# A meta-key split of its own, a row addition ahead of weight conversions, and a last accumulation ahead of another tile's output

## The chip, the cores and the metric

The kernel runs on one core of one Trainium2 chip. The metric is the device time of one execution in microseconds (us). The kernel before takes 1303.13 us, the median of 3 runs (1301.97 to 1304.59). One more execution was recorded with the hardware profiler; it took 1304.39 us, and its records span 1302.6 us.

## The reference

The reference is one encoder block over 16 learned meta tokens, a prompt of 512 rows and a sample of 256 rows, all of width 1024; both row groups use the same weights, and the meta rows are dropped from the output:

```
n1   = rmsnorm(h)
proj = n1 @ w_in                      # S5 input | q | k | v | retention gate | merge gates A, B
a    = GLU(gelu(S5(u)))               # bidirectional complex diagonal state
o    = retention(rope(q), rope(k), v) # 4 heads, chunkwise recurrent, both directions
state0[h] = sum_s km[s] vm[s] gf^(15-s)                # the 16 meta positions start the state
b    = (rmsnorm(o) * silu(gate)) @ w_ret_out
h    = h + (sigmoid(gate_a) * a + sigmoid(gate_b) * b) @ w_out
n2   = rmsnorm(h)
h    = h + (silu(n2 @ w_gate) * (n2 @ w_up)) @ w_ffn_out     # width 2816
out  = rmsnorm(h)[16:]
```

Three places of this matter here: the term `state0`, which needs the 16 meta keys of each head; the residual sum after `w_out` with the norm `n2` behind it; and the final norm.

## The kernel before

All matrix products run in a split form. An fp32 operand x is turned into a high part (`hi`, written by ScalarE, line 101, in the matmul type fp32r) and a low part (`lo` = x - hi, by VectorE or GpSimd, line 89), and a product is three matmuls: hi by hi, the cross term lo by hi, and hi by lo (lines 81, 82, 83 are one such triple; line 1114 is another place that issues them). Weights are converted 128 x 512 at a time by `convert` (line 162): `whi` on ScalarE, then `wlo` on VectorE. Converted weights lie in a ring of six pairs (`WH = 6`), raw weights in a ring of three tiles `wraw` (`WR = 3`). The class `Ops` (lines 178 to 196) is a queue over the conversions in a fixed sequence: `fill(n)` converts until n pairs wait in the queue, `next()` hands one out and fills up to `ahead` again. Some steps of the sequence carry a sum of weight quarters as well (`wraw<-wraw` on GpSimd), because the projections in pairs are done by a Strassen-Winograd scheme with seven products for eight; the operands `n20` to `n26` of the trace are the seven operands of that scheme on the activations.

Through nearly all of the program each engine works in the order in which the code is written (`manual_schedule`). An instruction that waits holds up all that stands behind it on its engine.

**Retention.** The four heads run from about 300 to 490 us. What one head does is a list of calls named by the string `SEQ` (line 48): `KS` splits the rotated keys, `VM` the meta values, `KT` turns the weighted keys and splits them, and also turns, weights and splits the 16 meta keys (`kmw`, `kmhi`, `kmlo`), `V0` to `V2` split the values (their low parts `vlo` on GpSimd), `ST` multiplies keys by values into the states, `S0` to `S2` form the scores (`sr`, then `sThi` and `sTlo`), and each `F` is one product of the gate projection, with the weight conversions that it causes and the copies and sums that take its result out of PSUM (`q`, `u`, `c`). The products `F` are not part of the retention; they fill TensorE while the head's own work goes through the other engines. `ws.ahead` is 4 here.

**Between w_out and the FFN.** The six row tiles of 128 rows take the second half of `w_out` one after the other (`col_half`, eight weight pairs `wos`, of which the first four lie in the ring and the last four in a pool of their own). After each tile its sum is added to the residual (`add_half`: `hres<-bank,hres`), ScalarE squares it (`row_stats`), GpSimd makes the reciprocal root, VectorE scales it (`scale_rows`: `nx<-hres,rstd,gffn`), TensorE transposes it (line 1877), and `rows_first` or `rows_second` form the FFN's operands from the transposed tile. Tile i is scaled inside the work on tile i - 1, at the place `mid`. In between the first FFN weights are converted by `ws.fill`. Then four products of FFN units 1 and 2 (`pre`), the last tile's transposes, and two products of unit 0 follow; from about 820 us the FFN proper runs.

**The end.** The last group of the FFN's second projection leaves three sums that arrive one after the other (i = 0, 1, 2). `accumulate(P4, i)` adds one to the residual, `second_half` takes the norm of row tile 3 + i, and `finish` scales a finished tile and issues its output DMAs. The last two outputs (`rows_out(5, ...)`) end the program.

Of the kernel before, what the change touches and what calls it, by code (L numbers as in the profile page):

```python
# [16 lines left out]
D = 1024  # L17
# [3 lines left out]
NT = SP + SS  # L21
NA = NT + NM
KT = D // 128
# [21 lines left out]
RS = ((1, 1, 1, 0), (1, 1, 1, 1), (1, 1, 0, 1), (1, 1, 1, 1))  # L45
DE = ((1, 1, 1, 1), (1, 1, 0, 1), (1, 1, 1, 1), (1, 1, 0, 1))
VLP = (0, 1, 2)
SEQ = 'B Z0 A D KS VM F V0 KL QD F C F F V1 F V2 KT S2 F F KU ST QL KR F F O2 S1 VL F Z2 F QU S0 O1 QR F DL Z1 QS F O0 F ZL'
HALF = 3.84
E_T = (0, 0.794)  # L50
R_T = (13, 0.997)
# [9 lines left out]
def build(nc, tc, I, O):  # L61
    V = nc.vector
    A = nc.scalar
    P = nc.gpsimd
    T = nc.tensor
# [11 lines left out]
    def raw(t):  # L77
        return t.bitcast(F32)
# [9 lines left out]
    def tt(e, out, a, b, op):  # L88
        e.tensor_tensor(out=out, in0=a, in1=b, op=op)  # L89

    def ts(e, out, a, s1, op0, s2=None, op1=None):
        if op1 is None:
            e.tensor_scalar(out=out, in0=a, scalar1=s1, scalar2=None, op0=op0)  # L93
        else:
            e.tensor_scalar(out=out, in0=a, scalar1=s1, scalar2=s2, op0=op0, op1=op1)  # L95
# [4 lines left out]
    def act(out, a, f, **kw):  # L100
        A.activation(out=out, in_=a, func=f, **kw)  # L101
# [40 lines left out]
    ident = cp.tile([128, 128], F32, name="ident")  # L142
# [71 lines left out]
    def weights():  # L214
        for i in range(NPLAIN):
            yield from plain(i, P if i == 3 else V)
        for i in range(12):
            yield from units.pop(i) if i in units else pair_unit(i)
        rq = [ret_unit(44 + 2 * i) for i in range(4)]
        for op in ("p1", "p5", "p2", "p3", "p6", "p7", "p4"):  # L220
            yield from (rq[0][op], rq[1][op])
        for u in rq[2:]:
            yield from (u[op] for op in ("p1", "p2", "p5", "p3", "p6", "p7", "p4"))
        for j in range(52, len(srcs)):
            yield from plain(j)
# [139 lines left out]
    ws = Ops(weights(), 0)  # L365
# [242 lines left out]
    rs = {}  # L608
# [496 lines left out]
    def bank():  # L1105
        banked[0] += 1
        return pb.tile([128, 512], F32, name="bank", tag="bank")
# [57 lines left out]
    st = [dict() for _ in range(H)]  # L1165

    def hilo(name, shape, src, eng=V, p=None):
        p = p or hp
        hi = p.tile(shape, F32R, name=name + "hi", tag=name + "hi")
        lo = p.tile(shape, F32R, name=name + "lo", tag=name + "lo")  # L1170
        act(hi, src, AF.Copy)
        tt(eng, lo, src, raw(hi), SUB)
        return hi, lo
# [20 lines left out]
    def k_load(h):  # L1194
        if h < H:
            st[h]["kr"], st[h]["ks"] = rotated(2 * h, NA)
            st[h]["kw"] = tab(h, "wk", 2, p=ha)
# [13 lines left out]
    def k_split(h):  # L1211
        st[h]["k"] = hilo("kT", [128, NT], st[h]["kr"][:, :NT])
# [22 lines left out]
    def q_decay(h):  # L1235
        qr, wq = st[h]["qr"], st[h]["wq"]
        tt(P, wq[:, 1], qr[:, 0:256], wq[:, 1], MUL)
        qf = qr.rearrange("p (n c) -> p n c", n=3)
        tt(P, qf, qf, wq[:, 0:1].to_broadcast([128, 3, 256]), MUL)
        st[h]["qf"], st[h]["qb"] = qf, wq[:, 1]  # L1240
# [11 lines left out]
    def v_load(h, i):  # L1252
        if h < H:
            st[h]["vr", i] = vr()
            nc.sync.dma_start(out=st[h]["vr", i], in_=vscr[h][:, 2 * VP[i]:2 * VP[i] + 2])

    def vm_split(h):
        vmr = st[h]["vmr"]
        tt(P, vmr[:, 0], vmr[:, 0], vmr[:, 1], ADD)
        st[h]["vm"] = hilo("vm", [16, DV], vmr[:, 0], p=ha)  # L1260
        v_load(h, 1)

    def v_split(h, i):
        if i == 0:
            st[h]["v"] = [hp.tile([128, 6, DV], F32R, name=n, tag=n) for n in ("vhi", "vlo")]
        j = 2 * VP[i]
        vhi, vlo = (x[:, j:j + 2] for x in st[h]["v"])
        act(vhi, st[h]["vr", i], AF.Copy)
        tt(P if i in VLP else V, vlo, st[h]["vr", i], raw(vhi), SUB)
        if i == 0:  # L1270
            v_load(h, 2)

    def k_states(h):
        kr, kwT = st[h]["kr"], st[h]["kwT"]
        ps = bank()
        for j in range(4):
            T.transpose(ps[:, j * 128:(j + 1) * 128], kwT[:, j * 128:(j + 1) * 128], ident)
        kw = hilo("kw", [128, 512], ps, p=ha)
        ps = bank()
        T.transpose(ps[:16, :128], kr[:, NT:], ident)  # L1280
        kmw = ha.tile([16, 128], F32, name="kmw", tag="kmw")
        ts(V, kmw, ps[:16, :128], wm[:, h:h + 1], MUL)
        st[h]["kw"] = kw
        st[h]["km"] = hilo("km", [16, 128], kmw, p=ha)

    def states(h):
# [231 lines left out]
    for h in range(H):  # L1518
        calls = {
            "KS": lambda: k_split(h), "VM": lambda: vm_split(h), "Z0": lambda: z_out(h - 1, 0) if h else 0,  # L1520
            "V0": lambda: v_split(h, 0), "KT": lambda: k_states(h), "QD": lambda: q_decay(h),
            "V1": lambda: v_split(h, 1), "V2": lambda: v_split(h, 2), "KL": lambda: k_load(h + 1),
            "S2": lambda: scores(h, 2), "VL": lambda: (vm_load(h + 1), v_load(h + 1, 0)),
            "ST": lambda: states(h), "KU": lambda: k_turn(h + 1), "KR": lambda: k_rope(h + 1),
            "O2": lambda: outs(h, 2), "S1": lambda: scores(h, 1), "QL": lambda: q_load(h + 1),
            "Z2": lambda: z_out(h, 2), "O1": lambda: outs(h, 1), "S0": lambda: scores(h, 0),
            "QU": lambda: q_turn(h + 1), "Z1": lambda: z_out(h, 1), "DL": lambda: dm_load(h + 1),
            "QR": lambda: q_rope(h + 1), "O0": lambda: outs(h, 0), "QS": lambda: q_split(h + 1), "F": f, "ZL": lambda: z_start() if h == H - 1 else 0,
            "A": lambda: t1_split(h, 0), "B": lambda: t1_split(h, 1), "C": lambda: t1_split(h, 2),
            "D": lambda: t1_split(h, 3),  # L1530
        }
        for name in SEQ.split():
            calls[name]()
# [318 lines left out]
    ws = Ops(weights_b(), WH - 2)  # L1852
# [78 lines left out]
    def row_stats(i):  # L1931
        nx = wx.tile([128, D], F32, name="nx2", tag="nx2", bufs=2)
        ss = wx.tile([128, 1], F32, name="ss", tag="ss", bufs=4)
        act(nx, hres[:, i], AF.Square, accum_out=ss)
        return nx, rstd_of(ss, D, wx)
# [11 lines left out]
    for i in range(6):  # L1947
        if i == 3:
            leave(mx_cms[1])
            n2pb_cm = pool("n2pb", side="right")  # L1950
            n2pb = enter(n2pb_cm)
            n2 += [[n2pb.tile([128, 4, 384], F32R, name=f"n2{op}{s}") for s in ("hi", "lo")]
                   for op in range(2, 7)]
        ps = col_half(i)
        if i == 4:
            ws.fill(2)
        if i == 5:
            ws.fill(6)
        add_half(i, ps)
        nxs[i] = row_stats(i)  # L1960
        if i == 0:
            scale_rows(0, *nxs[0])
        else:
            pt = rows_transposed(nxs[i - 1][0])
            mid = lambda: scale_rows(i, *nxs[i])
            if i - 1 < 3:
                rows_first(pt, i - 1, mid)
            else:
                rows_second(pt, i - 4, nxs[i - 1][0], mid)
    ws.fill(6)  # L1970
    pre = {(m, op): product(op, n2) for m in EARLY for op in (B11, B21)}
    ws.fill(4)
    pt = rows_transposed(nxs[5][0])
    rows_second(pt, 2, nxs[5][0], lambda: ws.fill(4))
    for op in (B11, B21):
# [28 lines left out]
    def h21(i):  # L2004
        return hres[:, 3 + i, 0:512]

    def h22(i):
        return hres[:, 3 + i, 512:1024]
# [247 lines left out]
    def finish(i, r, spare=False, qs=(0, 1)):  # L2256
        for q in qs:
            yo = row_tile()
            cs = slice(512 * q, 512 * q + 512)
            if spare:  # L2260
                act(yo, hres[:, i, cs], AF.Copy, scale=r[:, 0:1])
                tt(P, yo, yo, gfin[:, cs], MUL)
            else:
                stt(yo, hres[:, i, cs], r[:, 0:1], gfin[:, cs], MUL, MUL)
            rows_out(i, q, yo)
# [30 lines left out]
    rs = {}  # L2296
# [38 lines left out]
    for i in range(3):  # L2335
        ps = banks_of["u"][i]
        for k, w in enumerate(ks):
            product_rows(ps, i, w, False, k, len(g))
        if i == 0:
            upper_scales()  # L2340
            finish(1, rs[1], spare=True)
            finish(0, rs[0], qs=(0,))
        accumulate(P4, i, ps)
        rs[3 + i] = second_half(3 + i, h21(i))
        if i == 0:
            finish(0, rs[0], qs=(1,))
            finish(2, rs[2])
        if i == 1:
            finish(3, rs[3])
            tt(V, h22(2), h22(2), gfin[:, 512:], MUL)  # L2350
        elif i == 2:
            tt(V, h21(2), h21(2), gfin[:, 0:512], MUL)
            finish(4, rs[4])
    yo = [row_tile() for _ in range(2)]
# [106 lines left out]
```

## Time and profile before

| | |
|---|---|
| median of 3 runs | 1303.13 us |
| profiled execution, its own time | 1304.39 us |
| span of its records | 1302.6 us |
| TensorE matmul busy | 1213.6 us, 93% |
| VectorE busy | 944.2 us, 72% |
| ScalarE busy | 594.1 us, 46% |
| GpSimd busy | 626.5 us, 48% |
| mean granted TensorE clock | 0.968 |

The profiled execution is 1.26 us above the median and takes 1.8 us beyond its span. Engines are named PE (TensorE), DVE (VectorE), ACT (ScalarE) and POOL (GpSimd); SP issues the DMAs. A busy share says how much of the span an engine worked; what an engine waited for, and who was late, stands in the views of waits and in the timelines.

### The profile page before, as it was taken

How to read it: one execution, taken by the hardware profiler on the slowest of the kernel's cores; microseconds unless marked ns; L12 is line 12 of the kernel's file. 1: busy time of each engine (PE TensorE's matmuls, PEld its weight loads, DVE VectorE, ACT ScalarE, POOL GpSimd, SP SyncE). 2: the span in 40 equal slices, each digit the busy share in tenths (PEclk: the TensorE clock that was granted, in tenths of full speed). 3: DMA queues.
4: the chain of work that ended last, by engine and by line, in shares of the span. 5: the costliest groups of instructions: out<-in, count | busy, mean ns of one | idle time of the engine just before them, and what ended most of it. 6: DMA issues, size and time to landing. Idle time of an engine off the chain costs nothing. (4 is left out here: it accounts for less than half of the span.)

```text
span 1302.6 us, 19191 instructions
## 1 busy us (share of the span) xinstructions
PE 1213.6 (93%) x6821; PEld 1140.5 (88%) x6821; DVE 944.2 (72%) x1576; ACT 594.1 (46%) x1242; POOL 626.5 (48%) x607
## 2 busy tenths in 40 slices
PE   7899788998999999987899998999999999999996
PEld 7789678998888989976899887999999999888884
DVE  6997998558877776988544359766666656899897
ACT  5264344644354444343433235434444344468564
POOL 4306570536676655367355017544444444564174
PEclk8899899999999999998999999999999999999998
DMA  6351446766455434335342501333332222514002
GB/s 246 79 111 46 140 136 184 179 188 189 148 169 181 130 125 141 134 107 179 118 130 85 210 1 49 122 109 102 94 101 65 65 82 71 219 76 148 15 1 97
DMA packets 76736, 155.33 MB, mean 119 GB/s; under 512 B 18001, under 2 KB 37585, under 8 KB 76641
## 3 DMA queue, kind: packets, MB, share of 16 engines
q1 hardware_dynamic: 76640, 154.11, 37.9%
q8 instruction: 53, 0.87, 0.3%
q14 instruction: 43, 0.34, 0.1%
HBM read 118.50 MB, written 35.59 MB: 118 GB/s over the span
## 5 line engine op out<-in xcount | busy, mean ns | idle before, releaser
L89 DVE TENSOR_TENSOR wlo<-wraw,whi 128x512 fp32r<-128x512 f32 x298 | 246.1, 836 | 105.4 <-ACT whi L101 105.2
L101 ACT ACTIVATE whi<-wraw 128x512 fp32r<-128x512 f32 x304 | 183.6, 623 | 46.5 <-POOL wraw L89 14.5
L89 POOL TENSOR_TENSOR wraw<-wraw 128x512 f32<-128x512 f32 x93 | 130.0, 1398 | 141.8 <-DVE wlo L89 94.8
L89 POOL TENSOR_TENSOR wraw<-wrax,wraw 128x512 f32<-128x512 f32 x38 | 51.1, 1345 | 78.0 <-DVE wlo L89 44.3
L101 ACT ACTIVATE q<-bank 128x384 f32<-128x384 f32 x80 | 38.2, 484 | 66.1 <-PE bank L83 62.3
L83 PE MATMUL bank<-n1hi,wlo 128*128 128x384 f32 x192 | 66.3, 346 | 2.1 <-DVE wlo L89 2.1
L81 PE MATMUL bank<-n1hi,whi 128*128 128x384 f32 x192 | 67.5, 352 | 0.0
L82 PE MATMUL bank<-n1lo,whi 128*128 128x384 f32 x192 | 66.1, 344 | 0.0
L81 PE MATMUL pair<-n1hi,whi 128*128 128x384 f32 (+1 forms) x168 | 61.9, 369 | 3.1 <-ACT sgst L101 3.1
L82 PE MATMUL pair<-n1lo,whi 128*128 128x384 f32 (+1 forms) x168 | 59.8, 356 | 0.0
L83 PE MATMUL pair<-n1hi,wlo 128*128 128x384 f32 (+1 forms) x168 | 59.3, 353 | 0.0
L89 DVE TENSOR_TENSOR wlo<-wrax,whi 128x512 fp32r<-128x512 f32 x50 | 42.3, 853 | 17.8 <-ACT whi L101 17.8
L2293 PE MATMUL acc<-whi,ahi 128*128 128x512 f32 x132 | 52.4, 397 | 0.6 <-DVE hres L89 0.6
L2293 PE MATMUL acc<-wlo,ahi 128*128 128x512 f32 x132 | 52.3, 396 | 0.0
L2293 PE MATMUL acc<-whi,alo 128*128 128x512 f32 x132 | 52.3, 396 | 0.0
L89 DVE TENSOR_TENSOR X<-X,single 128x128 f32<-128x128 f32 (+2 forms) x128 | 42.9, 335 | 4.4
L89 POOL TENSOR_TENSOR er<-pwF,Cc 128x512 f32<-128x512 f32 x8 | 8.9, 1110 | 73.8 <-DVE pwF L566 42.9
L81 PE MATMUL bank<-yThi,whi 128*128 128x384 f32 x128 | 43.0, 336 | 0.0
L82 PE MATMUL bank<-yTlo,whi 128*128 128x384 f32 x128 | 43.0, 336 | 0.0
L83 PE MATMUL bank<-yThi,wlo 128*128 128x384 f32 x128 | 43.0, 336 | 0.0
L89 POOL TENSOR_TENSOR fr<-fr 128x384 f32<-128x384 f32 x29 | 36.1, 1251 | 13.4 <-DVE alo L89 12.9
L81 PE MATMUL pair<-whi,n1hi 128*128 128x256 f32 x144 | 41.3, 286 | 0.0
(517 smaller groups left out, 4284.6 us busy)
## 6 DMA issues: line engine op xcount, KB each, us to landing
wraw<-in_wfi SPq DMA_DIRECT2D x35, 512.0 KB, 3.7
wraw<-in_win SPq DMA_DIRECT2D x33, 512.0 KB, 5.3
w<-in_wfo SPq DMA_DIRECT2D x16, 512.0 KB, 4.6
wrax<-in_win SPq DMA_DIRECT2D x11, 512.0 KB, 4.4
wrax<-in_wfi SPq DMA_DIRECT2D x11, 512.0 KB, 3.6
fb<-fbscr SPq DMA_DIRECT2D x8, 512.0 KB, 4.4
wraw<-in_wo SPq DMA_DIRECT2D x8, 512.0 KB, 3.6
ffscr<-fr SPq DMA_DIRECT2D x10, 384.0 KB, 2.9
```

The source lines that it names most:

```text
L81: T.matmul(out, l[0], r[0], start=start, stop=False)
L82: T.matmul(out, l[0], r[1], start=False, stop=False)
L83: T.matmul(out, l[1], r[0], start=False, stop=stop)
L89: e.tensor_tensor(out=out, in0=a, in1=b, op=op)
L101: A.activation(out=out, in_=a, func=f, **kw)
L2293: T.matmul(ps, l[a], r[b], start=False, stop=False, skip_group_check=True)
```

## The change

There are three edits. First, the meta keys leave `k_states` for a function `k_meta`, called by a new name `KM` directly behind `VM` in every head. Second, in the stage between `w_out` and the FFN three weight pairs instead of two are converted ahead of row tile 4's addition; at row tile 5 the addition and the squares now stand ahead of the conversions, and only the queue's fourth pair is converted there; of the two fills behind the loop the second is gone. Third, near the end, `finish(3)` moves from behind the second of the three sums to behind the third.

```
-SEQ = '... KS VM F V0 KL QD F C F F V1 F V2 KT S2 F F KU ST ...'
+SEQ = '... KS VM KM F V0 KL QD F C F F V1 F V2 KT S2 F F KU ST ...'

     def k_states(h):
-        kr, kwT = st[h]["kr"], st[h]["kwT"]
+        kwT = st[h]["kwT"]
         ps = bank()
         for j in range(4):
             T.transpose(ps[:, j * 128:(j + 1) * 128], kwT[:, j * 128:(j + 1) * 128], ident)
-        kw = hilo("kw", [128, 512], ps, p=ha)
+        st[h]["kw"] = hilo("kw", [128, 512], ps, p=ha)
+
+    def k_meta(h):
         ps = bank()
-        T.transpose(ps[:16, :128], kr[:, NT:], ident)
+        T.transpose(ps[:16, :128], st[h]["kr"][:, NT:], ident)
         kmw = ha.tile([16, 128], F32, name="kmw", tag="kmw")
         ts(V, kmw, ps[:16, :128], wm[:, h:h + 1], MUL)
-        st[h]["kw"] = kw
         st[h]["km"] = hilo("km", [16, 128], kmw, p=ha)
...
         if i == 4:
-            ws.fill(2)
-        if i == 5:
-            ws.fill(6)
+            ws.fill(3)
         add_half(i, ps)
         nxs[i] = row_stats(i)
+        if i == 5:
+            ws.fill(4)
...
     ws.fill(6)
     pre = {(m, op): product(op, n2) for m in EARLY for op in (B11, B21)}
-    ws.fill(4)
     pt = rows_transposed(nxs[5][0])
     rows_second(pt, 2, nxs[5][0], lambda: ws.fill(4))
...
         if i == 1:
-            finish(3, rs[3])
             tt(V, h22(2), h22(2), gfin[:, 512:], MUL)
         elif i == 2:
+            finish(3, rs[3])
             tt(V, h21(2), h21(2), gfin[:, 0:512], MUL)
             finish(4, rs[4])
```

On DVE a head of the retention reads as follows, before. `vmlo` ends the split of the meta values; `kmw` and `kmlo` are the meta keys; `wlo` are weight conversions, and the sums `c` and `u` belong to the products `F`; `sr` is the first step of the scores.

```order
L89 TENSOR_TENSOR vmlo<-vr,vmhi 16x256
L89 TENSOR_TENSOR wlo<-wraw,whi 128x512 x2
L89 TENSOR_TENSOR c<-bank,q_4567 128x384
L89 TENSOR_TENSOR wlo<-wraw,whi 128x512
L89 TENSOR_TENSOR u_4568<-bank,q_4567 128x384
L89 TENSOR_TENSOR wlo<-wraw,whi 128x512
L89 TENSOR_TENSOR c<-bank,u_4568 128x384
L89 TENSOR_TENSOR wlo<-wraw,whi 128x512
L89 TENSOR_TENSOR u_4569<-bank,u_4568 128x384
L89 TENSOR_TENSOR kwlo<-bank,kwhi 128x512
L93 TENSOR_SCALAR kmw<-bank,wm 16x128
L89 TENSOR_TENSOR kmlo<-kmw,kmhi 16x128
```

The same place of the changed kernel on DVE:

```order
L89 TENSOR_TENSOR vmlo<-vr,vmhi 16x256
L93 TENSOR_SCALAR kmw<-bank,wm 16x128
L89 TENSOR_TENSOR kmlo<-kmw,kmhi 16x128
L89 TENSOR_TENSOR wlo<-wraw,whi 128x512 x2
L89 TENSOR_TENSOR c<-bank,q_4575 128x384
L89 TENSOR_TENSOR wlo<-wraw,whi 128x512
L89 TENSOR_TENSOR u_4576<-bank,q_4575 128x384
L89 TENSOR_TENSOR wlo<-wraw,whi 128x512
L89 TENSOR_TENSOR c<-bank,u_4576 128x384
L89 TENSOR_TENSOR wlo<-wraw,whi 128x512
L89 TENSOR_TENSOR u_4577<-bank,u_4576 128x384
L89 TENSOR_TENSOR kwlo<-bank,kwhi 128x512
```

The pair `kmw`, `kmlo` moved from the end of this stretch to its beginning, ahead of the first two weight conversions; ACT's `kmhi`, which reads `kmw` and feeds `kmlo`, moved with it.

On ACT, in the stage between `w_out` and the FFN, from row tile 4 on, before. `nx,ss<-hres` are the squares of a row tile, `whi` the conversions, `n22hi` to `n26hi` and `b` the operands made of the tile before.

```order
L101 ACTIVATE whi<-wraw 128x512 x2
L101 ACTIVATE nx_8143,ss<-hres 128x1024
L101 ACTIVATE n22hi<-nx_8079 128x4x128
L101 ACTIVATE b_7978<-bank 128x512
L101 ACTIVATE n23hi<-nx_8079 128x4x128
L101 ACTIVATE n24hi<-bank 128x4x128
L101 ACTIVATE n25hi<-xc 128x4x128
L101 ACTIVATE n26hi<-xc 128x4x128
L101 ACTIVATE whi<-wraw 128x512 x4
L101 ACTIVATE nx_8233,ss<-hres 128x1024
L101 ACTIVATE n22hi<-nx_8143 128x4x128
```

The same place of the changed kernel on ACT:

```order
L101 ACTIVATE whi<-wraw 128x512 x3
L101 ACTIVATE nx_8149,ss<-hres 128x1024
L101 ACTIVATE n22hi<-nx_8079 128x4x128
L101 ACTIVATE b_7978<-bank 128x512
L101 ACTIVATE n23hi<-nx_8079 128x4x128
L101 ACTIVATE n24hi<-bank 128x4x128
L101 ACTIVATE n25hi<-xc 128x4x128
L101 ACTIVATE n26hi<-xc 128x4x128
L101 ACTIVATE nx_8215,ss<-hres 128x1024
L101 ACTIVATE whi<-wraw 128x512
L101 ACTIVATE n22hi<-nx_8149 128x4x128
```

A third conversion now stands ahead of tile 4's squares; tile 5's squares come before one conversion where they came behind four. The two conversions that are left moved further down, to where the last two of the stage stood.

On DVE at the end of the program, the piece of the difference; `hres<-acc` are the last two accumulations, `yq<-hres,rstd,gffn` the scaled outputs of finished tiles:

```order
 L89 TENSOR_TENSOR hres<-acc_12489,hres 128x512
-L98 SCALAR_TENSOR_TENSOR yq<-hres,rstd,gffn 128x512 x2
 L89 TENSOR_TENSOR hres<-hres,gffn 128x512
 L89 TENSOR_TENSOR hres<-acc_12490,hres 128x512
+L98 SCALAR_TENSOR_TENSOR yq<-hres,rstd,gffn 128x512 x2
 L89 TENSOR_TENSOR hres<-hres,gffn 128x512
```

Two output scalings, which wait for a reciprocal root from POOL, stand behind the last accumulation where they stood ahead of it.

## Rows read from the trace of the kernel before

**Rows 1.** Stretches: us, busy us of each engine (instructions), granted clock, DMA share, GB/s.
```profile
780.00:820.00 40.00, 33.21 (x173) 30.02 (x173) 37.27 (x43) 20.38 (x39) 28.84 (x26) 0.96 0.14 45
820.00:1280.00 460.00, 457.98 (x2379) 427.25 (x2377) 334.83 (x504) 236.08 (x460) 207.20 (x154) 1.00 0.27 89
```

**Rows 2.** PE's waits in the retention: us in total, times, longest us.
```profile
PE bank L81 <- ACT kmhi L101: 10.2, 4, 2.6
```

**Rows 3.** DVE's waits in one head, from 376 to 424 us.
```profile
DVE wlo L89 <- ACT whi L101: 5.0, 5, 1.8
```

**Rows 4.** DVE timeline, second head: start us, us, instruction, [idle before <- who ended it].
```profile
364.63 0.67 DVE L89 TENSOR_TENSOR wlo<-wraw,whi 128x512 fp32r<-128x512 f32 x1
365.97 1.36 DVE L89 TENSOR_TENSOR wlo<-wraw,whi 128x512 fp32r<-128x512 f32 x1 [0.67 <-ACT whi L101]
...
375.08 0.33 DVE L93 TENSOR_SCALAR kmw<-bank,wm 16x128 f32<-16x128 f32 x1
...
376.52 0.67 DVE L89 TENSOR_TENSOR sr<-bank,dm 128x512 f32<-128x512 f32 x1
377.89 0.69 DVE L89 TENSOR_TENSOR sTlo<-sr,sThi 128x512 fp32r<-128x512 f32 x1 [0.70 <-ACT sThi L101]
```

**Rows 5.** ACT timeline, second head.
```profile
363.91 0.62 ACT L101 ACTIVATE whi<-wraw 128x512 fp32r<-128x512 f32 x1
...
375.45 0.31 ACT L101 ACTIVATE kmhi<-kmw 16x128 fp32r<-16x128 f32 x1 [3.95 <-DVE kmw L93]
```

**Rows 6.** POOL timeline, second head.
```profile
373.50 2.94 POOL L89 TENSOR_TENSOR vlo<-vr,vhi 128x512 fp32r<-128x512 f32 x2
376.41 1.32 POOL L89 TENSOR_TENSOR wraw<-wraw 128x512 f32<-128x512 f32 x1
```

**Rows 7.** PE timeline, second head, in the states.
```profile
378.33 0.41 PE L82 MATMUL bank<-vlo,kwhi 128*128 128x256 f32 x1
```

**Rows 8.** ACT timeline, first head.
```profile
315.27 0.61 ACT L101 ACTIVATE whi<-wraw 128x512 fp32r<-128x512 f32 x1
```

**Rows 9.** DVE timeline, first head.
```profile
316.93 1.27 DVE L89 TENSOR_TENSOR wlo<-wraw,whi 128x512 fp32r<-128x512 f32 x2
```

**Rows 10.** PE timeline, between w_out and the FFN.
```profile
782.52 0.39 PE L83 MATMUL bank<-whi,mx2lo 128*128 128x512 f32 x1
...
787.80 1.06 PE L1877 MATMUL bank<-ident,nx 128*128 128x128 f32 x8
```

**Rows 11.** PE timeline, same stage, last row tile.
```profile
800.84 1.94 PE L1877 MATMUL bank<-ident,nx 128*128 128x128 f32 x8 [3.50 <-DVE nx L98]
...
803.22 0.52 PE L83 MATMUL bank<-n20hi,wlo 128*128 128x384 f32 x1
```

**Rows 12.** DVE timeline, same stage.
```profile
781.38 0.69 DVE L89 TENSOR_TENSOR hres<-bank,hres 128x512 f32<-128x512 f32 x1
...
790.97 3.58 DVE L89 TENSOR_TENSOR wlo<-wraw,whi 128x512 fp32r<-128x512 f32 x4
794.47 0.68 DVE L89 TENSOR_TENSOR hres<-bank,hres 128x512 f32<-128x512 f32 x1
795.07 0.68 DVE L89 TENSOR_TENSOR nx<-bank,b 128x512 f32<-128x512 f32 x1
...
798.42 2.27 DVE L98 SCALAR_TENSOR_TENSOR nx<-hres,rstd,gffn 128x1024 f32<-128x1024 f32 x1 [0.20 <-POOL rstd L89]
...
803.99 2.38 DVE L89 TENSOR_TENSOR wlo<-wraw,whi 128x512 fp32r<-128x512 f32 x2
```

**Rows 13.** ACT timeline, same stage.
```profile
795.23 1.06 ACT L101 ACTIVATE nx<-hres 128x1024 f32<-128x1024 f32 x1 [3.69 <-issue]
```

**Rows 14.** DVE timeline, end of the program.
```profile
1293.92 0.68 DVE L89 TENSOR_TENSOR hres<-acc,hres 128x512 f32<-128x512 f32 x1
```

**Rows 15.** POOL timeline, end of the program.
```profile
1294.31 0.27 POOL L95 TENSOR_SCALAR rstd<-rtmp,rstd 128x1 f32<-128x1 f32 x1
1295.51 0.76 POOL L95 TENSOR_SCALAR rvar<-fss 128x1 f32<-128x1 f32 x1 [0.93 <-ACT yo L101]
```

More of the change, by code (lines that the diff above doesn't have):

```diff
@@ L47 @@
 VLP = (0, 1, 2)
-SEQ = 'B Z0 A D KS VM F V0 KL QD F C F F V1 F V2 KT S2 F F KU ST QL KR F F O2 S1 VL F Z2 F QU S0 O1 QR F DL Z1 QS F O0 F ZL'
+SEQ = 'B Z0 A D KS VM KM F V0 KL QD F C F F V1 F V2 KT S2 F F KU ST QL KR F F O2 S1 VL F Z2 F QU S0 O1 QR F DL Z1 QS F O0 F ZL'
 HALF = 3.84
@@ L1273, in k_states @@
     def k_states(h):
-        kr, kwT = st[h]["kr"], st[h]["kwT"]
+        kwT = st[h]["kwT"]
         ps = bank()
@@ L1277, in k_states, with k_meta @@
             T.transpose(ps[:, j * 128:(j + 1) * 128], kwT[:, j * 128:(j + 1) * 128], ident)
-        kw = hilo("kw", [128, 512], ps, p=ha)
+        st[h]["kw"] = hilo("kw", [128, 512], ps, p=ha)
+    def k_meta(h):
         ps = bank()
-        T.transpose(ps[:16, :128], kr[:, NT:], ident)
+        T.transpose(ps[:16, :128], st[h]["kr"][:, NT:], ident)
         kmw = ha.tile([16, 128], F32, name="kmw", tag="kmw")
         ts(V, kmw, ps[:16, :128], wm[:, h:h + 1], MUL)
-        st[h]["kw"] = kw
         st[h]["km"] = hilo("km", [16, 128], kmw, p=ha)
@@ L1520, in build @@
             "KS": lambda: k_split(h), "VM": lambda: vm_split(h), "Z0": lambda: z_out(h - 1, 0) if h else 0,
-            "V0": lambda: v_split(h, 0), "KT": lambda: k_states(h), "QD": lambda: q_decay(h),
+            "V0": lambda: v_split(h, 0), "KT": lambda: k_states(h), "KM": lambda: k_meta(h), "QD": lambda: q_decay(h),
             "V1": lambda: v_split(h, 1), "V2": lambda: v_split(h, 2), "KL": lambda: k_load(h + 1),
@@ L1955, in build @@
         if i == 4:
-            ws.fill(2)
-        if i == 5:
-            ws.fill(6)
+            ws.fill(3)
         add_half(i, ps)
         nxs[i] = row_stats(i)
+        if i == 5:
+            ws.fill(4)
         if i == 0:
@@ L1971, in build @@
     pre = {(m, op): product(op, n2) for m in EARLY for op in (B11, B21)}
-    ws.fill(4)
     pt = rows_transposed(nxs[5][0])
@@ L2348, in build @@
         if i == 1:
-            finish(3, rs[3])
             tt(V, h22(2), h22(2), gfin[:, 512:], MUL)
         elif i == 2:
+            finish(3, rs[3])
             tt(V, h21(2), h21(2), gfin[:, 0:512], MUL)
```

## The prediction

> **What bounds the kernel now.** I read the table of stretches first. From 820 to 1280 us PE works 457.98 of 460 us: nothing there can take up a delay or add one, so whatever a stage ahead of 820 us loses or gains comes out at the end. Between 780 and 820 us PE works only 33.21 of 40 us while DVE works 37.27: there DVE sets the pace [rows 1]. So I ask of each edit what it does to the engine that paces its stage, and only then what it does to PE.
>
> In the retention the list of PE's waits has one large entry: PE waits four times, once per head, for `kmhi`, 10.2 us in all [rows 2]. That is tempting: the first edit makes `kmhi` some ten microseconds earlier in each head. But the waits of DVE over a whole head name ACT (five waits of `wlo` for `whi`, 5.0 us) and not PE [rows 3]. DVE, ACT and POOL wait for one another and run behind PE; PE runs ahead, is stopped once per head at the states, and runs ahead again. A wait removed from PE there does not add up over the heads; what adds up is how long the three engines need per head. PE keeps a gain only at the last head, where the last of these four stops stands.
>
> **Meta keys.** Per head one transpose on PE, `kmw` and `kmlo` on DVE and `kmhi` on ACT move; no DMA does. In the old place the piece on DVE lasts from `kmw` at 375.08 to `sr` at 376.52, 1.44 us [rows 4], and POOL works on two `vlo` until 376.44 beside it [rows 6], so it cost POOL nothing. In the new place it stands between `vmlo` and the first weight conversion, and ACT's `kmhi`, which waits for `kmw`, stands ahead of `whi` and everything behind that. DVE reaches the place at 364.63, when the first `wlo` started [rows 4]; `kmhi` follows `kmw` by 375.45 - 375.08 = 0.37 us and takes about 0.22 us until the next may start (an estimate, under its 0.31), so `whi` starts at 365.22 instead of 363.91 [rows 5]: 1.31 us later. Queued behind it are ACT's `vhi`, POOL's `vlo` that waits for that, and DVE's second `wlo`, which waited for ACT before too [rows 4]. The three engines arrive at the scores 1.31 us late and save 1.44 there: -0.13 us.
>
> Then one thing is late that was hidden: POOL's second `vlo` ends at 377.75 instead of 376.44, so POOL's next sum, 1.32 us long, which ran from 376.41 to 377.73 while DVE waited [rows 6], now runs beside `sTlo` and the `wlo` behind it. A `wlo` with POOL beside it took 1.36 us, one without 0.67 [rows 4]: +0.69. Together +0.56 per head. I take that for the second and third head.
>
> This case's rows show a DVE instruction of two SBUF inputs about doubled beside POOL, as just used [rows 4]. The Trainium skill, "SBUF — State Buffer", section "Who interferes with whom", has it stronger: such an instruction contends with a GpSimd one that reads SBUF, and whoever issues first makes the other wait for its whole length. The doubled `wlo` agrees. By that rule the whole 1.32 us would be lost per head, 1.19 net, and the retention would come to +2.7; I keep the row's 0.69.
>
> In the first head ACT is further ahead of DVE: its `whi` starts at 315.27 [rows 8], DVE reaches the place at 316.93 [rows 9], so `whi` would start at 316.93 + 0.59 = 317.52, 2.25 us late; less 1.44 this is +0.8. In the last head PE's states wait no longer for `kmhi` but for the third key tile's `vlo`: 377.75 against 378.33, when PE used it before [rows 7]; PE gains about 0.5. Sum: 0.8 + 2 x 0.56 - 0.5 = **+1.4 us**. Ends: if the three engines absorb the piece in their own waits, each head gains 1.44, -5.8; if PE's waits were what paced the stage, all 10.2 would go; if POOL's sum blocks fully, +2.7.
>
> **Between w_out and the FFN.** The third conversion ahead of tile 4's addition takes a slot of the ring. Six pairs: four are held by the first `wos`, two by the pairs just converted. The slot it needs is that of the first `wos`, whose last reader is the first triple of tile 5's `col_half`, which ends at 782.52 + 0.39 = 782.91 [rows 10]. So ACT's third `whi` waits until then, ends at 783.53 (0.62 [rows 5]), and DVE's third `wlo` (0.67) waits for it. Behind that `wlo` stands tile 4's addition, which ran at 781.38 [rows 12]: now about 784.20. DVE idles 783.53 - 781.38 = 2.15 us, and tile 4's squares, root, scaling and transposes follow 2.8 us late: the transposes at 787.80 [rows 10] come at about 790.6 and PE waits.
>
> Tile 5's addition no longer stands behind four conversions of 3.58 us [rows 12]: it starts where the first of them would, 790.97 + 2.82 = 793.79, against 794.47, only 0.7 earlier. Then comes the fourth conversion: its `whi` stands behind the squares (1.06 us [rows 13]), so DVE's `wlo` waits 1.06 + 0.62 + some 0.07 of hand-over = 1.75 us, and what stands behind it on DVE (the operands of tile 4 and the scaling of tile 5) starts at 793.79 + 0.68 + 1.75 + 0.67 = 796.89 instead of 795.07: +1.8. The last transposes come at 802.6 instead of 800.84 [rows 11]. The wait of 3.50 us there, which the edit is about, shrinks for PE because PE itself is late.
>
> Then unit 0's first pair is converted in the place of the 2.38 us pair at 803.99 [rows 12]: its first `wlo` ends near 803.99 + 1.8 + 1.19 = 807.0, and PE asks for it at 803.22 + 1.8 = 805.0 [rows 11]: 2.0 more. The next two conversions go into the last tile's operands. DVE has the same conversions to do before 820 us as before and paces the stage, so the stage loses DVE's new idle time, 2.15 + 1.75 = **+3.9 us**. Ends: 4 x 0.67 for the 3.58 us of conversions if they no longer run beside POOL saves 0.9 and all idle is covered, -0.9; the second pair of 2.38 wholly on the path, +6.3.
>
> **End.** `finish(3)` leaves the path of the last accumulation, which ran at 1293.92 [rows 14]. It and its squares no longer stand behind two scalings and their wait for a root, so they are done before POOL asks for them; but POOL is busy with the root of tile 4 until 1294.31 + 0.27 = 1294.58, and only then starts tile 5's, which began at 1295.51 [rows 15]: **-0.9 us**; the chain behind it to the last output keeps its length, and tile 3's output, now behind the accumulation, is two scalings and a DMA that still start ahead of tile 5's. Ends: 0, and -1.4 if POOL's first step takes 0.27 like the row above it instead of 0.76.
>
> **Sum.** +1.4 + 3.9 - 0.9 = +4.4. Against the profiled execution's 1304.39 that is 1308.8; that execution stands 1.26 above the median, so against the median of 1303.1 it is **1307.5 us**.
>
> **Rivals.**
> - The piece is absorbed (faster). DVE's waits for `whi` in a head, 5.0 us [rows 3], take the new piece if ACT, by running ahead, still delivers each `whi` no later than DVE asks. It decides whether the first `wlo` behind `vmlo` starts late and the second does not. Then -5.8 + 3.9 - 0.9 = -2.8: 1300.3. For it: ACT idles much of the head (3.95 us before `kmhi` alone [rows 5]). Against it: the second `wlo` waits for ACT already [rows 4], and ACT would wait for DVE at `kmhi`.
> - The third conversion finds a slot (no measurable change). If the ring has room, the 2.15 us do not arise and the stage costs 1.75 - 0.9 = 0.85: +1.4 + 0.85 - 0.9 = 1.4, 1304.5. For it: only that the order alone does not show slots. Against it: the count of pairs above.
> - The clock falls behind the new waits (slower still). Behind the 3.50 us wait the granted speed showed: eight transposes took 1.94 us against 1.06, and a matmul of 384 columns 0.52 [rows 10, 11]. Taking 0.88 for the transposes and as much again for the triples behind them, some 1.6 us, at each of two new waits (tile 4's transposes, unit 0's first product): +3.2, total +7.6, 1310.7.
>
> **Chances.** A change of under 0.2% (2.6 us) can't be told from none in this kernel. Forecast 0.46, absorbed 0.18, slot found 0.17, clock 0.19. Faster by over 2.6 us is most of the absorbed case and a little of mixtures, 0.20; within it the slot case and the lower edge of the forecast, 0.22; slower 0.58. The range, 1299.5 to 1312.0, holds the cases down to the absorbed one and leaves out the ends -0.9 and -10.2 of the terms taken together, and the sum of all upper ends.
>
> **What would show it.** Retention: PE's wait for `kmhi` gone, the period from head to head longer by about half a microsecond, and a `whi` late by 1.3 us behind `kmhi`. Then: a gap of DVE of about 2 us ahead of a third `wlo` near 781.4 (in times of before), transposes of tile 4 with a wait of near 3 us, a gap of 1.75 us behind tile 5's addition, and a wait of about 2 us in unit 0's first product. End: the last accumulation without a wait between it and the one before, and tile 5's root directly behind tile 4's. I am wrong if the period of a head is shorter than before, or if tile 4's addition stays at its place behind `col_half`.

## The result, and the profile after

The changed kernel takes 1310.72 us (median of 4 runs, 1308.63 to 1311.64) against 1302.55 us before (median of 4, 1301.96 to 1304.59): a ratio of 1.0055, with a 95% interval of 1.0042 to 1.0068, so between 5.5 and 8.9 us slower. The profiled execution took 1310.84 us, 6.45 more than the one of before. By the medians it is 8.2: the profiled execution of before lay 1.84 us above its median, the changed one 0.12 above its own.

To see where these lie, I cut the profiles at the same five events: the start of the first head's `vmlo`, the last matmul of the last head's states, the first transpose of line 1877 (1878 or 1879 where a kernel has lines added above it), the first matmul that reads `n24hi`, and the last matmul. The table has the start of the first event and then the time between each event and the next, in us; the last column ends with the start of the last output scaling on ACT. It holds all ten kernels of this study, to which the later sections come back.

```
                              to 1st   1st vmlo   states to   1st tr. to   n24hi to   last mm to
kernel                         vmlo    to states  1st transp.   n24hi       last mm   last scaling
before                        316.59    157.33     288.22       53.24       475.21      7.82
changed                       317.66    160.83     287.18       57.36       475.21      6.60
meta keys alone               313.69    161.34     289.32       53.24       475.20      7.78
fills alone                   315.33    158.10     288.32       57.34       475.86      7.77
end alone                     317.16    157.46     288.18       53.22       475.21      6.58
fills, two conversions        315.73    157.32     286.71       55.12       475.23      7.82
split without kmw             315.07    154.91     287.23       53.22       475.23      7.82
split without kmw, early      316.07    155.97     288.28       53.23       475.23      7.81
addition between conversions  315.38    157.16     286.92       54.31       475.23      7.81
split without kmw, and end    317.04    154.98     287.29       53.23       475.23      6.62
```

The first and third columns hold nothing that any of these kernels changes in its own work there, and they scatter by 4.0 and 2.6 us; they are most of what makes one execution differ from another. Among kernels that are alike there, the second column repeats to 0.3 us (0.5 between the two with the first edit, 0.8 in one of five like before), the fourth and the sixth to 0.05, the fifth to 0.05 but for one ("fills alone", where ten matmuls from 820.58 us on took 0.52 us each instead of 0.34). Each row is one execution. So the change costs 160.83 - 157.33 = 3.5 us in the retention and 57.36 - 53.24 = 4.1 us between `w_out` and the FFN, and gives 7.82 - 6.60 = 1.2 us back at the end: +6.4. The rest of the 6.45 is +1.07 ahead of the first head and -1.04 in the third column.

**Retention.** PE's waits between 300 and 490 us in the changed kernel (us in total, times, longest us), where `kmhi` stood first with 10.2 [rows 2]:

```profile
PE bank L82 <- POOL vlo L89: 6.9, 6, 1.7
PE bank L86 <- ACT S L101: 2.7, 3, 1.7
PE bank L83 <- DVE wlo L89: 2.5, 2, 1.4
PE bank L81 <- ACT whi L101: 1.9, 2, 1.6
```

The wait for `kmhi` is gone, and PE stands instead in the same states, for POOL's `vlo`, and elsewhere for ACT. The second head on DVE, changed kernel, answering to [rows 4]:

```profile
366.99 0.41 DVE L89 TENSOR_TENSOR vmlo<-vr,vmhi 16x256 fp32r<-16x256 f32 x1
367.32 0.33 DVE L93 TENSOR_SCALAR kmw<-bank,wm 16x128 f32<-16x128 f32 x1
368.03 0.28 DVE L89 TENSOR_TENSOR kmlo<-kmw,kmhi 16x128 fp32r<-16x128 f32 x1 [0.38 <-ACT kmhi L101]
368.55 0.69 DVE L89 TENSOR_TENSOR wlo<-wraw,whi 128x512 fp32r<-128x512 f32 x1 [0.24 <-ACT whi L101]
...
379.03 0.67 DVE L89 TENSOR_TENSOR sr<-bank,dm 128x512 f32<-128x512 f32 x1
380.41 1.80 DVE L89 TENSOR_TENSOR sTlo<-sr,sThi 128x512 fp32r<-128x512 f32 x1 [0.70 <-ACT sThi L101]
```

ACT at the place where the piece now stands, answering to [rows 5]:

```profile
366.28 0.42 ACT L101 ACTIVATE vmhi<-vr 16x256 fp32r<-16x256 f32 x1 [0.65 <-POOL vr L89]
367.69 0.31 ACT L101 ACTIVATE kmhi<-kmw 16x128 fp32r<-16x128 f32 x1 [0.99 <-DVE kmw L93]
367.90 0.61 ACT L101 ACTIVATE whi<-wraw 128x512 fp32r<-128x512 f32 x1
```

And POOL at the scores, answering to [rows 6]:

```profile
377.46 2.96 POOL L89 TENSOR_TENSOR vlo<-vr,vhi 128x512 fp32r<-128x512 f32 x2
380.37 1.30 POOL L89 TENSOR_TENSOR wraw<-wraw 128x512 f32<-128x512 f32 x1
```

In the kernel before, the two instructions from which the next sentences count stand at

```profile
363.59 0.42 ACT L101 ACTIVATE vmhi<-vr 16x256 fp32r<-16x256 f32 x1 [0.65 <-POOL vr L89]
364.30 0.41 DVE L89 TENSOR_TENSOR vmlo<-vr,vmhi 16x256 fp32r<-16x256 f32 x1
```

Read them together. `whi` starts 1.62 us behind `vmhi`, before it was 0.32; that is the late start of ACT. `sr` nevertheless comes 12.04 us behind `vmlo`, against 12.22 before: what is lost ahead of the conversions is saved behind them. Then POOL's sum, which began 1.48 us ahead of `sTlo` before (376.41 and 377.89), begins 0.04 us ahead of it, and `sTlo` takes 1.80 us instead of 0.69. It does so in all four heads (1.80 or 1.81).

**Between w_out and the FFN.** DVE in the changed kernel, answering to [rows 12]; the gaps are in brackets:

```profile
787.22 0.69 DVE L89 TENSOR_TENSOR wlo<-wraw,whi 128x512 fp32r<-128x512 f32 x1 [2.33 <-ACT whi L101]
787.83 0.68 DVE L89 TENSOR_TENSOR hres<-bank,hres 128x512 f32<-128x512 f32 x1
...
797.36 0.68 DVE L89 TENSOR_TENSOR hres<-bank,hres 128x512 f32<-128x512 f32 x1
799.83 0.69 DVE L89 TENSOR_TENSOR wlo<-wraw,whi 128x512 fp32r<-128x512 f32 x1 [1.79 <-ACT whi L101]
...
814.22 2.92 DVE L89 TENSOR_TENSOR wlo<-wraw,whi 128x512 fp32r<-128x512 f32 x2 [1.25 <-ACT whi L101]
```

The stops of PE in the same stage, answering to [rows 10, 11]:

```profile
794.20 1.06 PE L1878 MATMUL bank<-ident,nx 128*128 128x128 f32 x8 [2.97 <-DVE nx L98]
804.89 1.06 PE L1878 MATMUL bank<-ident,nx 128*128 128x128 f32 x8 [1.15 <-DVE nx L98]
807.12 0.44 PE L81 MATMUL bank<-n20hi,whi 128*128 128x384 f32 x1 [1.16 <-ACT whi L101]
809.83 0.69 PE L83 MATMUL bank<-n20hi,wlo 128*128 128x384 f32 x1 [2.11 <-DVE wlo L89]
```

The third `whi`, for which the first of these gaps of DVE waits, starts at 786.55 us, 0.09 us behind the end of the first triple of tile 5's `col_half` (786.46). The profile names no releaser for it; the time fits the wait for the ring's slot.

The 3.50 us wait of the last row tile went down to 1.15, as the edit's order says it should; 2.97 us of waiting came up at the tile before and 3.3 us in the product behind. From the first pair of `wlo` of this stage to the first sum `c` behind it DVE needs 33.00 us before (from 780.05) and 37.12 us now (from 783.60); its waits within it sum to 1.93 and 6.02 us. The longer time is idle time.

**End.** The last accumulation on DVE is the second `hres<-acc` here; before, it ran 3.33 us behind the last matmul (1290.59, 1293.92 [rows 14]), now 0.93 (1298.24):

```profile
1297.95 0.68 DVE L89 TENSOR_TENSOR hres<-acc,hres 128x512 f32<-128x512 f32 x1
1298.55 0.70 DVE L89 TENSOR_TENSOR hres<-hres,gffn 128x512 f32<-128x512 f32 x1
1299.17 0.68 DVE L89 TENSOR_TENSOR hres<-acc,hres 128x512 f32<-128x512 f32 x1
```

POOL between tile 4's root and tile 5's, answering to [rows 15]; the gap of 0.93 us is closed:

```profile
1302.20 0.27 POOL L95 TENSOR_SCALAR rstd<-rtmp,rstd 128x1 f32<-128x1 f32 x1
1302.44 0.27 POOL L95 TENSOR_SCALAR rvar<-fss 128x1 f32<-128x1 f32 x1
```

### The profile page after: what moved, and what is told of

The parts are those of the page before. It is cut to its first block, busy times and chain, and to the rows that moved or that the text cites. A ratio compares the mean times of both kernels' runs of the same rounds, so it can differ in the third digit from the quotient of the medians.

```text
span 1309.1 us, 19194 instructions
## 1 busy us (share of the span) xinstructions
PE 1216.1 (93%) x6821; PEld 1138.5 (87%) x6821; DVE 947.8 (72%) x1576; ACT 594.9 (45%) x1242; POOL 625.4 (48%) x607
## 4 chain that ended last, share of the span: by engine, by line
PE 46%; DVE 4%; POOL 3%; issue 2%; ACT 1%; DMA 0%; POOLq 0%; DVEq 0%; ACTq 0%
PE bank L1114 14%; PE bank L83 7%; PE bank L81 7%; PE bank L82 7%; PE acc L2293 6%; PE acc L81 2%; PE acc L83 2%; PE acc L82 2%; DVE wlo L89 1%; POOL xc L89 1%; POOL sgb L89 0%; ACT whi L101 0%; POOL rstd L89 0%; POOL wraw L89 0%; DVE nx L89 0%
## 5 line engine op out<-in xcount | busy, mean ns | idle before, releaser
L95 POOL TENSOR_SCALAR rvar<-ss 128x1 f32<-128x1 f32 (+1 forms) x13 | 5.4, 412 | 75.6 <-ACT nx L101 68.1
```

## Experiments

The first four take the change apart; all ran in turn with the kernel before on one chip (median 1303.01 there).

**The first edit alone.**

```
-SEQ = '... KS VM F V0 ...'
+SEQ = '... KS VM KM F V0 ...'      # with k_meta, as in the change; nothing else
```

> The first edit alone: the meta keys split right behind the meta values in every head, all else as before. Theory (the three lane engines ACT, DVE and POOL set the length of a head; PE's wait for kmhi is only where PE meets them): about +2.5 us, since in the changed kernel the first head lost 0.75 us up to its first score and each head another 1.1 us at sTlo, which ran 1.80 us beside POOL instead of 0.69. Rival (PE's waits for kmhi, 10.2 us in all, pace the stage): 5 to 10 us faster. Rival (the loss of the whole change is elsewhere): 0 within 1 us.

Measured: 1309.29 us, ratio 1.0043 (1.0031 to 1.0055), 4.0 to 7.2 us slower. In the profile the retention is 161.34 - 157.33 = 4.0 us longer. The periods of the heads (from one `vmlo` to the next) grew by 1.87, 1.21 and 0.90 us, the rest up to the last states by nothing. The sign and the place are the first theory's; the size is not, it is half as much again or more. The second theory is out, the kernel is slower: PE's wait for `kmhi` is gone here too, and in its place stands

```profile
PE bank L82 <- POOL vlo L89: 7.2, 7, 1.7
```

Why the runs say more than the retention's 4.0 us is not settled: the profiled execution (1306.57 us) was the shortest of the five, and where the others lose more no profile shows.

**The second edit alone.**

```
         if i == 4:
-            ws.fill(2)
-        if i == 5:
-            ws.fill(6)
+            ws.fill(3)
         add_half(i, ps)
         nxs[i] = row_stats(i)
+        if i == 5:
+            ws.fill(4)
...                                  # and the second fill behind the loop gone
```

> The second edit alone: three conversions ahead of row tile 4's addition, tile 5's addition and squares ahead of one conversion, the later fills as in the changed kernel. Theory (DVE sets the pace between 780 and 820 us and gets two new idle times, 2.3 us ahead of the third wlo and 1.8 us behind tile 5's addition): +4.1 us. Rival (PE's 3.5 us wait for the last tile's scaling sets the pace; it shrinks to 1.15 us): 2 us faster. Rival (the clock falls behind the new waits): +6 or more.

Measured: 1307.11 us, ratio 1.0035 (1.0022 to 1.0048), 2.9 to 6.3 us slower; the stage takes 57.34 us, 4.1 more. The first theory's number. The last tile's wait is gone altogether here, its transposes start without one, and that buys nothing, which rules the second out. The clock is out as well: in this profile, other than in the changed kernel's, the eight transposes behind the 2.97 us wait did slow, to 1.94 us, and the granted clock of the stage was 0.94 instead of 0.97, yet the stage is as long as there, 57.34 against 57.36 us. By the runs alone, up to 6.3 us, the clock's +6 would not be excluded.

**The third edit alone.**

```
         if i == 1:
-            finish(3, rs[3])
...
         elif i == 2:
+            finish(3, rs[3])
```

> The third edit alone: the scaling of row tile 3 behind the last accumulation. Theory (POOL's chain of roots limits the gain; tile 5's root starts right behind tile 4's): -1.2 us, the last accumulation some 2 us earlier. Rival (the last accumulation itself sets the end): -2.3 us. Rival (the end is set by the output DMAs): 0.

Measured: 1302.34 us, ratio 0.9996 (0.9987 to 1.0004): by its time it can't be told from nothing, from -1.7 to +0.5 us. The profile is sharper: from the last matmul to the last scaling 6.58 us instead of 7.82, -1.24, the first theory's number.

**Two conversions ahead of tile 4 instead of three.**

```
         if i == 4:
-            ws.fill(3)
+            ws.fill(2)
```

> The second edit with two conversions instead of three ahead of row tile 4's addition (as before the change there), all else of that edit kept: two conversions then stand behind tile 5's squares. Theory (each idle time of DVE counts by itself; only the one ahead of the third wlo, 2.3 us, goes): +1.8 us against before, tile 4's transposes without a wait. Rival (the third conversion's wait for a slot of the ring is the whole cost): 0 to -2 us. Rival (it is the late conversions of units 0's operands that cost, not the idle time): +4.

Measured: 1305.53 us, ratio 1.0021 (1.0013 to 1.0030), 1.7 to 3.9 us slower than before; the stage takes 55.12 us, 1.9 more than before and 2.2 less than with three. So each idle time counts by itself, as the theory had it (+1.8): the wait for a slot of the ring is worth its 2.3 us, and the order behind tile 5's addition costs the other 1.9. PE's waits between 770 and 840 us, largest first:

```profile
PE bank L83 <- DVE wlo L89: 2.1, 1, 2.1
PE bank L1114 <- ACT q L101: 1.7, 1, 1.7
PE bank L81 <- ACT whi L101: 1.5, 2, 1.2
PE bank L1877 <- DVE nx L98: 0.8, 1, 0.8
```

There is no wait any more at tile 4's transposes, 0.8 us is left of the last tile's 3.5, and still the stage is longer than before.

The next four ask what the meta keys would be worth in another form, and what the wait of 3.5 us is worth. They ran in turn with the kernel before, whose median was 1302.97 there.

**The meta keys split without kmw, old place.**

```
-        kmw = ha.tile([16, 128], F32, name="kmw", tag="kmw")
-        ts(V, kmw, ps[:16, :128], wm[:, h:h + 1], MUL)
-        st[h]["km"] = hilo("km", [16, 128], kmw, p=ha)
+        kmh, kml = ...                # two tiles of type fp32r
+        act(kmh, ps[:16, :128], AF.Copy, scale=wm[:, h:h + 1])
+        stt(kml, ps[:16, :128], wm[:, h:h + 1], raw(kmh), MUL, SUB)
+        st[h]["km"] = (kmh, kml)
```

> The kernel before with the meta keys in their old place, but split without kmw: ACT writes kmhi from PSUM with the weight as its scale, and DVE forms kmlo in one operation (PSUM times weight minus kmhi). kmhi then follows ACT's kwhi at once, so PE's four waits for it (10.2 us) go, and DVE saves about 1.1 us per head (kmw 0.33, its wait 0.38, half of kmlo). Theory (the lane engines set a head's length, and the last states then wait for POOL's vlo; DVE's 1.1 us are taken back where sTlo meets POOL's sum, which ends at 377.73 as before): -1.4 us at the last head and about -0.1 per other head, -1.7 in all. Rival (PE's waits pace the stage): -5 to -10. Rival (DVE alone paces it): -4.4.

Measured: 1302.37 us, ratio 0.9996 (0.9987 to 1.0005), from -1.7 to +0.6 us. By the profile the retention is 2.4 us shorter, which lies outside the runs' interval; the profiled execution (1299.48 us) was the shortest of the eleven, and what the others lose is not shown. Runs and profile both exclude the first rival, of 5 to 10 us, and the second, of 4.4. But PE's wait was not taken away, it changed its name: where PE stood for `kmhi` it now stands, two matmuls later, for

```profile
PE bank L83 <- DVE kmlo L98: 7.1, 4, 1.9
```

and its idle time between the first two events of the table is 12.8 us, against 12.4 before. The second head on DVE:

```profile
373.19 0.33 DVE L98 SCALAR_TENSOR_TENSOR kmlo<-bank,wm,kmhi 16x128 fp32r<-16x128 f32 x1
373.45 0.67 DVE L89 TENSOR_TENSOR sr<-bank,dm 128x512 f32<-128x512 f32 x1
374.82 1.55 DVE L89 TENSOR_TENSOR sTlo<-sr,sThi 128x512 fp32r<-128x512 f32 x1 [0.70 <-ACT sThi L101]
```

POOL beside it:

```profile
374.53 1.29 POOL L89 TENSOR_TENSOR wraw<-wraw 128x512 f32<-128x512 f32 x1
```

DVE saves its microsecond, arrives at `sTlo` while POOL's sum runs (until 375.82), and `sTlo` ends at 376.37, 0.55 us behind the sum. In the changed kernel it ended at 382.21, 0.54 us behind the sum's 381.67. The same distance for two different starts: `sTlo` gets on only when the sum is done. In the kernel before it ended 0.85 us behind the sum (377.73 and 378.58 [rows 4, 6]), so 0.30 us is all that an earlier DVE can gain here while POOL's sum stays where it is. The heads' period is 47.3 to 47.4 us against 47.4 to 47.7: a head got up to 0.3 us shorter, not 1.1. The other 1.65 us of the 2.4 come behind the last head's `vmlo`. Of these 0.45 are the clock: from the matmul with `kmlo` to the last of the states PE takes 1.71 us, against 2.16 before, where the last six matmuls took 0.39 to 0.41 us instead of 0.28 (granted clock of the 15 to 17 us around them 1.00, before 0.91).

**The same split in the new place.**

```
-SEQ = '... KS VM F V0 ...'
+SEQ = '... KS VM KM F V0 ...'      # KM as above: kmhi on ACT with scale, kmlo in one DVE operation
```

> The first edit alone in the same split without kmw: kmhi right behind vmhi on ACT, kmlo behind vmlo on DVE, no wait of ACT for DVE. Theory (what the first edit cost was ACT's wait for kmw, 1.3 us in a head and 2.25 in the first, and behind it POOL's sum colliding with sTlo): ACT is late by one small instruction only, about 0.25 us, so POOL's sum ends near its old time: 0 within 1 us against before, and 4 to 5 us faster than the first edit alone. Rival (the place costs, whatever stands in it): +3 or more.

Measured: 1301.97 us, ratio 0.9994 (0.9985 to 1.0003): the same as before, and 7.3 us below the first edit alone (each against its own runs of before: -1.0 and +6.3). The place with this split costs nothing on balance. ACT in the second head:

```profile
363.04 0.42 ACT L101 ACTIVATE vmhi<-vr 16x256 fp32r<-16x256 f32 x1 [0.69 <-POOL vr L89]
363.36 0.34 ACT L101 ACTIVATE kmhi<-bank,wm 16x128 fp32r<-16x128 f32 x1
363.61 0.62 ACT L101 ACTIVATE whi<-wraw 128x512 fp32r<-128x512 f32 x1
```

`whi` follows `vmhi` by 0.57 us; with `kmw` between it was 1.62. The time is the theory's, one step of it is not. The sum of POOL still meets `sTlo` in full, here and in the other three heads:

```profile
376.15 1.81 DVE L89 TENSOR_TENSOR sTlo<-sr,sThi 128x512 fp32r<-128x512 f32 x1 [0.70 <-ACT sThi L101]
376.13 1.28 POOL L89 TENSOR_TENSOR wraw<-wraw 128x512 f32<-128x512 f32 x1
```

DVE pays for it with what it saves ahead (`sr` comes 11.03 us behind `vmlo`, against 12.22), and the periods are 47.62 to 47.68 us, as in the kernels that leave the meta keys alone (47.4 to 47.7). So the meeting alone does not make a head longer. What the first edit costs is the hand-over from DVE to ACT at a place where ACT feeds POOL: its `whi` starts 1.05 us later than here, and its second and third periods are 1.0 us longer.

**Tile 5's addition between the conversions.**

```
         if i == 5:
-            ws.fill(6)
+            ws.fill(4)
         add_half(i, ps)
...
-            mid = lambda: scale_rows(i, *nxs[i])
+            mid = lambda: (scale_rows(i, *nxs[i]), ws.fill(6) if i == 5 else 0)
```

> The kernel before, between w_out and the FFN, with tile 5's addition behind two conversions instead of four and the other two behind tile 5's scaling: the addition comes 1.7 us earlier without any wait for a slot and without a conversion behind the squares. Theory (DVE has the same work before 820 us and paces the stage): PE's wait of 3.5 us shrinks by about 1.5, and the FFN starts at the old time, 0 to -0.5 us. Rival (PE's wait for the last tile's scaling paces the stage): -1.5.

Measured: 1303.74 us, ratio 1.0006 (0.9997 to 1.0015); the stage takes 54.31 us, 1.1 more. PE's wait for the last tile fell from 3.5 to 1.2, and a wait of 4.4 us for `b` came up behind it. The rival is out; my theory's number is off by one microsecond, and DVE shows why: the two conversions now run beside two sums of POOL.

```profile
795.67 3.45 DVE L89 TENSOR_TENSOR wlo<-wraw,whi 128x512 fp32r<-128x512 f32 x2
```

```profile
796.84 3.41 POOL L89 TENSOR_TENSOR wraw<-wraw 128x512 f32<-128x512 f32 x2
```

Four `wlo` took 3.58 us before [rows 12]; here two take 3.45.

**Split without kmw in the old place, and the third edit.** The two diffs above together.

> The split without kmw in the old place, and the third edit (the scaling of row tile 3 behind the last accumulation). If the two add up: -1.7 - 1.2 = -2.9 us against before. Rival (the third edit is worth nothing): -1.7.

Measured: 1300.39 us, ratio 0.9979 (0.9970 to 0.9988), 1.6 to 3.9 us faster than before. They add up, as expected (-2.6 by the medians; by the profile -2.35 and -1.20). It is faster than the kernel before and than the changed one; of its two parts neither could be told from nothing by its time alone.

The three edits of the change, each alone, sum to +6.3 + 4.1 - 0.7 = +9.7 us by the medians, against +8.2 for the change, which the intervals allow. By the stages they changed they sum to 4.0 + 4.1 - 1.2 = +6.9 us, against +6.4.

## Why the prediction came out as it did

The direction was right, the measured 1310.7 lies in the range, and each edit had the sign that was forecast; the size was short, +4.4 against 5.5 to 8.9. That 1310.7 is also the figure of the rival with the clock is chance: its mechanism did not add to the time.

*The stages set by the other engines.* Right. In the retention PE's 10.2 us of waiting for `kmhi` went away in five kernels, and each time PE waited 6.8 to 7.2 us for another tile instead (`vlo` or `kmlo`), with +3.5 (the change), +4.0 (the first edit alone), -2.4 and -2.35 (the split without `kmw`, alone and with the third edit) and -1.4 us (that split in the new place) in the stage. The stage did not follow PE's wait for `kmhi`; a kernel in which PE's idle time itself shrinks was not run. Between `w_out` and the FFN PE's 3.5 us wait was shortened four ways (to 1.15, 0.8 and 1.2, and to nothing with the fills alone), and the stage became longer each time.

*Meta keys, +1.4.* This is the term that was mis-sized; it measured +3.5. The step up to the scores was right: `whi` 1.30 us late (1.31 forecast), `sr` 0.18 us early against `vmlo` (0.13). The step behind it failed in size: "+0.69" for the work that now runs beside POOL's sum, taken from a `wlo` that took 1.36 instead of 0.67. Measured: 1.80 - 0.69 = 1.11 us, in each head. And I left it out of the first head, where only 0.8 stood. The periods from one `vmlo` to the next grew by 1.62, 1.18 and 1.00 us, where I had 0.8, 0.56 and 0.56; the last head, where I gave PE 0.5 us, gave 0.3. ACT, POOL and DVE make one chain here: where DVE arrives while POOL's sum runs, `sTlo` ends 0.55 us behind the sum, and the sum comes as late as ACT started. So a head's period should change by ACT's lateness less the 0.30 us by which `sTlo` ended later than that behind the sum before. That gives +1.00, -0.05 and -0.30 us for `whi` late by 1.30, 0.25 and 0 us (the change, the split in the new place, the split in the old place), where the second and third periods changed by 1.18 and 1.00, by 0.20 and -0.05, and by -0.11 and -0.31 (among kernels alike there the second scatters by 0.27, the third by 0.05). What the first head would have been without the collision is near what I said: its first `sr` came 1.82 us late, less the 1.07 of its start, 0.75.

The rule of the Trainium skill that I set beside this term ("SBUF — State Buffer", section "Who interferes with whom": whoever issues first makes the other wait for its whole length) was nearer than my row: it gave 1.19 net per head, 1.18 and 1.00 were measured in the second and third; for the retention it gave +2.7 of the +3.5, the rest is mainly the first head's collision. The `wlo` of 1.36 us [rows 4] was a poor measure: POOL's `vlo` beside it had started 0.47 us earlier, so that `wlo` had only the rest of it to wait out, and ended 0.54 us behind it; `sTlo` met nearly the whole sum. In the kernel before:

```profile
365.50 1.29 POOL L89 TENSOR_TENSOR vlo<-vr,vhi 128x512 fp32r<-128x512 f32 x1 [1.94 <-ACT vhi L101]
```

*Between w_out and the FFN, +3.9.* Right, +4.1. Each of its steps was found: a gap of 2.33 us ahead of the third `wlo` (2.15 forecast), 2.97 us of waiting at tile 4's transposes (2.8), a gap of 1.79 us behind tile 5's addition (1.75), 2.11 us in unit 0's first product (2.0). Not foreseen were 1.16 us of PE waiting for `whi` just ahead of that and a third gap of DVE of 1.25 us at 814.22, ahead of the two conversions that moved into the last tile's operands. In exchange DVE no longer waits 0.73 us in that tile and 0.40 + 0.20 us in the one before. That these cancel is luck: the sum has neither.

*End, -0.9.* Right, -1.2. The limit is the one named, POOL's chain: tile 5's root starts where tile 4's ends. Beyond the gap of 0.93 us the first step is shorter, 0.27 us instead of 0.76, as the end of -1.4 had it; against it tile 4's root ends 0.24 us later behind the last matmul than before.

*Rivals.* The piece is not absorbed: the periods are longer. The third conversion finds no slot: the gap is there, and the kernel with two conversions has none of it. The clock didn't add to it: the eight transposes behind the 2.97 us wait took 1.06 us, as those without a wait, and from `n24hi` to the last matmul the changed kernel takes 475.21 us as before. Behind the other new wait, of 2.11 us, it did fall: seven matmuls of 384 columns took 0.52 us each from 810.32 us on. But the slow matmuls behind the 3.50 us wait of before are gone in exchange (the last tile's transposes take 1.06 us instead of 1.94), and the granted clock from the first transpose to `n24hi` is 0.97 in both kernels.

## What to carry to other kernels

In this kernel a long wait of TensorE was not worth its length: with the tile it named made early, TensorE waited for the next late one. Where three engines wait for one another and TensorE meets them once per round, measure the round, not the wait. Before work is put in front of a conversion, ask which buffer the conversion needs and who frees it, and what stands behind it on its engine: here one slot of a ring held up a residual addition for 2.3 us. When a small operation that goes from one engine to a second and back is moved, ask which engines it shifts against each other: in its old place it held up DVE by 1.44 us and POOL not at all, in the new one ACT and POOL behind it by 1.3 us; without the first hand-over from DVE to ACT it could stand in either place.

## What the runs showed of the hardware

A VectorE operation of 128 x 512 on two SBUF inputs that started while a GpSimd operation on SBUF ran ended 0.54 to 0.55 us behind that operation's end: `sTlo` of 0.69 us took 1.80 us started 0.04 us behind GpSimd's sum and 1.55 us started 0.29 us behind it, `wlo` 1.36 us started 0.47 us behind `vlo`. Where VectorE's operation was first, by 0.01 us, it took its usual time, and GpSimd's sum 1.82 us, where one of the same shape shortly before took 1.30. In the kernel before:

```profile
862.07 0.68 DVE L89 TENSOR_TENSOR wlo<-wraw,whi 128x512 fp32r<-128x512 f32 x1
862.08 1.82 POOL L89 TENSOR_TENSOR wrax<-wrax 128x512 f32<-128x512 f32 x1
```

Two `wlo` beside two sums took 3.45 us, where a pair alone took 1.28.

Executions of one program differ by up to 4 us in the first 317 us and by 2.6 us between the states and the first transposes, while the stages between them repeat to 0.05 to 0.5 us, with single exceptions up to 0.8. A change of 1 us, which eleven whole runs couldn't tell from nothing, can be read between two events of the profile; but a profile is one execution, and that of the split without `kmw` shows more than the runs bear out.
